# A two-layer decoder trunk on one core: the first hi row written by the modulating operation, and the rotary part of attention in fewer vector operations

## The chip, the cores and the metric

One core of a Trainium2 chip runs the whole program in one launch. The metric is device time in microseconds (us) of that core. TensorE (PE), VectorE (DVE), ScalarE (ACT) and GpSimd (POOL) each execute their own instruction list in order and wait for each other through semaphores; SyncE (SP) issues the DMA transfers.

## The reference, cut to what matters

256 tokens of width 1024 pass through two layers. Each layer is a SwiGLU FFN, a block of three attentions side by side (MLA with 6 heads, a sliding-window attention, a stick-breaking attention), and a second SwiGLU FFN. Ahead of each stands an RMS norm whose output is scaled and shifted by vectors that are computed from a conditioning vector. The part that the change touches is the MLA head preparation:

```python
h = modulate(x, norm_g[l, 0], sh1, sc1)              # rms_norm(x) * (1 + scale) + shift
...
qa = (rms_norm(c_q, q_a_norm[l]) @ w_uq[l]).reshape(B, S, MLA_HEADS, MLA_QK)   # 6 heads of 64 + 32
qa = rms_norm(qa, mla_q_norm[l])
qa = jnp.concatenate([qa[..., :MLA_NOPE], rope(qa[..., MLA_NOPE:], positions)], axis=-1)
kv = (rms_norm(c_kv, kv_a_norm[l]) @ w_ukv[l]).reshape(B, S, MLA_HEADS, MLA_NOPE + MLA_V)
k_pe_h = jnp.broadcast_to(k_pe[:, :, None, :], (B, S, MLA_HEADS, MLA_ROPE))
ka = rms_norm(jnp.concatenate([kv[..., :MLA_NOPE], k_pe_h], axis=-1), mla_k_norm[l])
ka = jnp.concatenate([ka[..., :MLA_NOPE], rope(ka[..., MLA_NOPE:], positions)], axis=-1)
```

`rope` turns the two halves (16 and 16) of the 32 rotary columns of a head by an angle: `[x1*cos - x2*sin, x2*cos + x1*sin]`.

## The kernel before, in words

The large matmuls run in three passes on pairs of tiles: an fp32 operand is split into a rounded "hi" part and the remainder "lo", and hi·hi, lo·hi and hi·lo are added up in PSUM (lines 243, 246 and 247, in `mm3`). The weights come in through SP as `raw`, ACT or DVE writes `hi` (line 230), DVE writes `lo` (line 234). The activations have their own pair: `hh` and `hl`, eight rows of 128 features by 256 tokens. Between its other work DVE forms the conditioning vectors, one 128x1024 product-and-sum after another (line 171).

A scheduler of the language decides the order of the instructions on each engine from the order in the program, the dependencies and its own estimate of durations; what is wrapped in `pin` keeps its place in program order. Two instructions of different engines that touch one PSUM tile are put one after the other, even where both only read.

**The opening** (lines 1205 to 1241) makes the first row of the first FFN's input: DVE multiplies row 0 of x by the norm factor (line 1236), applies scale and shift (1237), rounds the result to `hh[:, 0]` (1239), subtracts to get `hl[:, 0]` (1240), and copies the norm factor (1241). Then come the `lo` parts of the first weights (234) and the further rows, one by one, in `opening` (lines 451 to 462).

**Attention** first projects to the MLA latents. Line 797 multiplies to `kps`, the unscaled keys and values of all heads: four PSUM tiles, one for each block `b` of 128 tokens and each half `hf` of the heads. They take all four slots of the PSUM pool `mm`. ACT squares the key parts (844) and copies the value parts (855), DVE sums the squares (845), POOL takes the power -1/2 to get `rk` (848). DVE turns the shared rotary key `kpe` of each block by a call of `rope` (lines 832 to 838). Then, for each `b` and `hf`, PE makes three query heads of 96 columns in a PSUM tile (line 863), ACT copies the 64 plain columns to `qcat` (866), DVE turns the 32 rotary columns (four operations: 835 to 838), ACT squares all 96 columns (869) and DVE sums the squares (870). DVE then makes `rkn` (875), scales the plain keys into `kcat` (879; each of these four is the last reader of one tile of `kps`) and the rotary keys (880). DVE puts together the variance of the queries (884), POOL takes the power (886), DVE scales it (888). PE transposes `qcat` and `kcat` by heads (900) into tiles of the pool `mm`; ACT copies the queries out to `qT` (903), DVE the keys to `kT` (905). The scores of MLA (1058), and with them the rest of attention, follow. In both layers PE has one more projection (`stick_in(1, 4)`, 48 matmuls of lines 243 to 247) beside these steps.

Of the kernel before, what the change touches and what calls it, by code (L numbers as in the profile page):

```python
# [7 lines left out]
F32 = mybir.dt.float32  # L8
# [4 lines left out]
AF = mybir.ActivationFunctionType  # L13
ALU = mybir.AluOpType
AX = mybir.AxisListType

P = 128
# [36 lines left out]
def trunk_kernel(ctx: ExitStack, tc: tile.TileContext, x, c, posc, positions, cols_in, row, w_mod, w_gu1, w_down1, w_in,  # L54
                 w_small, w_out, w_gu2, w_down2, out):
    nc = tc.nc
    pin = tc.keep_in_program_order
    ACT, DVE, POOL, PE, SP = nc.scalar, nc.vector, nc.gpsimd, nc.tensor, nc.sync
# [19 lines left out]
    xa = res.tile([P, KD, T], F32, name="xa")  # L78
# [4 lines left out]
    hh, hl = (h[:, 0:KD * T].rearrange("p (k t) -> p k t", k=KD) for h in (h_hi, h_lo))  # L83
# [69 lines left out]
    modc = const.tile([P, 2, 9, 8], F32, name="modc")  # L153
# [491 lines left out]
    def attention(l, ap, aw, bg):  # L645
# [13 lines left out]
        def spread(a, n):  # L659
            return a.rearrange("p (h o) -> p h o", o=1).to_broadcast([P, a.shape[-1], n])  # L660

        def over_heads(a, n):
            return a.rearrange("p (o d) -> p o d", o=1).to_broadcast([P, n, a.shape[-1]])
# [83 lines left out]
        def stick_in(i, at):  # L747
            if C["L"][l]["U"][i] == at:
                banks[i] = [pacc(), pacc()]
                drain(unscaled(3328 + 2048 * i, (P, P), banks[i], 1))  # L750
                left = banks.copy()
                for j in left if len(left) == 2 else ():
                    stick_out(j)
                if len(outs) == 4:
                    norm(l, 1, rsb)
# [74 lines left out]
        ksq = ap.tile([P, 2, 6, 64], F32, tag="s5", name="ksq")  # L830

        def rope(dst, src, tb, n, nm):
            ta = aw.tile([P, n, 32], F32, tag="ropa" + nm, name="ropa")
            t2 = aw.tile([P, n, 32], F32, tag="ropb" + nm, name="ropb")
            DVE.tensor_tensor(ta, src, over_heads(tb[:, 0:32], n), op=ALU.mult)
            DVE.tensor_tensor(t2[:, :, 0:16], src[:, :, 16:32], over_heads(tb[:, 32:48], n), op=ALU.mult)
            DVE.tensor_tensor(t2[:, :, 16:32], src[:, :, 0:16], over_heads(tb[:, 48:64], n), op=ALU.mult)
            DVE.tensor_tensor(dst, ta, t2, op=ALU.add)

        kv = ap.tile([P, 2, 6], F32, name="kv")  # L840
        krs = []
        for b in range(2):
            for hf in range(2):
                ACT.activation(ksq[:, b, hf * 3:hf * 3 + 3], kps[2 * b + hf][:, :, 0:64], AF.Square)
# [1 line left out]
            DVE.tensor_scalar(kv[:, b], kss[:, b], lr2[:, 1, b:b + 1], kpss[:, b:b + 1], op0=ALU.mult, op1=ALU.add)  # L846
        rk = kv
        POOL.tensor_tensor(rk.rearrange("p b h -> p (b h)"), kv.rearrange("p b h -> p (b h)"), nhalf[:, 0:12], op=ALU.pow)
        for b in range(2):
            krs.append(aw.tile([P, 1, 32], F32, tag="kr", name="kr"))  # L850
            rope(krs[b], kpe[:, b:b + 1], ropet[:, l, 1, b], 1, "k")
        for b in range(2):
            for hf in range(2):
                hs = slice(hf * 3, hf * 3 + 3)
                ACT.activation(va[:, b, hs], kps[2 * b + hf][:, :, 64:128], AF.Copy, scale=lr[:, 1, b:b + 1])
        stick_in(0, 3)
        stick_in(1, 3)
        for b in range(2):
            for hf in range(2):
                hs = slice(hf * 3, hf * 3 + 3)  # L860
                qp = pacc()
                for k in range(2):
                    PE.matmul(qp[:, 0:288], cT[:, k, b * P:(b + 1) * P], wuq[:, k, hf * 288:(hf + 1) * 288],
                              start=k == 0, stop=k == 1)
                q3 = heads3(qp[:, 0:288])
                ACT.activation(qcat[:, b, hs, 0:64], q3[:, :, 0:64], AF.Copy)
                rope(qcat[:, b, hs, 64:96], q3[:, :, 64:96], ropet[:, l, 0, b], 3, "q")
                sq = aw.tile([P, 3, 96], F32, tag="pr", name="qsq")
                ACT.activation(sq, q3, AF.Square)
                DVE.tensor_reduce(qss[:, b, hs], sq, axis=AX.X, op=ALU.add)  # L870
                stick_in(0, 10 + 2 * b + hf)
                stick_in(1, 10 + 2 * b + hf)
        rkn = ap.tile([P, 2, 6], F32, name="rkn")
        for b in range(2):
            DVE.tensor_scalar(rkn[:, b], rk[:, b], lr[:, 1, b:b + 1], None, op0=ALU.mult)
        for b in range(2):
            for hf in range(2):
                hs = slice(hf * 3, hf * 3 + 3)
                DVE.tensor_tensor(kcat[:, b, hs, 0:64], kps[2 * b + hf][:, :, 0:64], spread(rkn[:, b, hs], 64), op=ALU.mult)
            DVE.tensor_tensor(kcat[:, b, :, 64:96], krs[b].to_broadcast([P, 6, 32]), spread(rk[:, b], 32), op=ALU.mult)  # L880

        qv = ap.tile([P, 2, 6], F32, name="qv")
        for b in range(2):
# [350 lines left out]
    pin(mod_tile(0, 0, 0, m0[:, 0]))  # L1234
    mod_finish(0, 0, 2, slice(0, 1))
    pin(DVE.tensor_tensor(xa[:, 0], xT[:, 0], rb, op=ALU.mult))
    pin(DVE.tensor_scalar(xa[:, 0], xa[:, 0], modc[:, 0, 1, 0:1], modc[:, 0, 0, 0:1], op0=ALU.mult, op1=ALU.add))
    rb0 = wk.tile([P, T], F32, tag="rsb", bufs=1, name="rsb")
    pin(DVE.tensor_copy(hh[:, 0], xa[:, 0]))
    pin(DVE.tensor_tensor(hl[:, 0], xa[:, 0], hh[:, 0].bitcast(F32), op=ALU.subtract))  # L1240
    pin(DVE.tensor_copy(rb0, rb))
    for l in range(DEPTH):
# [112 lines left out]
```

## Time and profile before

| | us |
|---|---|
| median of 3 runs | 1007.82 |
| lowest and highest of the 3 | 1006.34 and 1023.81 |
| the profiled execution, its own time | 1007.52 |
| span of the profiled execution | 1005.6 |

The rows further down come from the profiled execution: its span, 1005.6 us, runs from the first to the last instruction, and 1.9 us of its own time lie around it. Starts are counted from the start of the span. Where the text speaks of the spacing of two instructions it means start to start, since two neighbours on one engine can overlap a little.

### The profile page before, as it was taken

Reading aid. Unit: us, or ns where it says so; the run is one execution under the profiler, and the core shown is the slowest. Engines: PE = TensorE matmul, PEld = TensorE weight load, DVE = VectorE, ACT = ScalarE, POOL = GpSimd, SP = SyncE. Lnnn points to the kernel's source line nnn. Section 1 sums busy time; section 2 is a strip of 40 time slices with the busy share of each in tenths; the row PEclk is TensorE's granted clock in tenths of the full one; section 3 lists DMA queues with packets and bytes.
Section 4 is the critical chain, followed back from the end, with each engine's and each line's share of the span. In section 5 each row is a group of like instructions: output and inputs, shape, how many; then the busy total and the mean of one; then the engine's idle time right before and its main releaser. Section 6 shows DMA issues by size and latency. Waiting matters only on the chain.

```text
span 1005.6 us, 20450 instructions
## 1 busy us (share of the span) xinstructions
PE 983.7 (98%) x8396; PEld 957.1 (95%) x8396; DVE 792.2 (79%) x1422; ACT 533.3 (53%) x951; POOL 76.6 (8%) x123
## 2 busy tenths in 40 slices
PE   7999999998999999999999999999999999999998
PEld 6999999997888999999999999999988899999998
DVE  6999788898886898888789877777886678566663
ACT  4464345465755764444376444446575666444442
POOL 6001503002010000000000000000110000000000
PEclk9999999999999999999999999999999999999999
DMA  9988998654661679888866887772443146566631
GB/s 347 414 299 340 296 371 329 271 189 137 224 238 49 244 275 394 340 354 339 348 217 240 335 300 295 273 285 95 127 146 112 58 181 240 194 228 248 224 114 43
DMA packets 47936, 245.13 MB, mean 244 GB/s; under 512 B 4193, under 2 KB 4961, under 8 KB 29666
## 3 DMA queue, kind: packets, MB, share of 16 engines
q1 hardware_dynamic: 47840, 243.81, 64.9%
q8 instruction: 66, 1.08, 0.4%
q14 instruction: 28, 0.23, 0.1%
q10 hardware_dynamic: 2, 0.00, 0.0%
HBM read 242.69 MB, written 1.11 MB: 242 GB/s over the span
## 4 chain that ended last, share of the span: by engine, by line
PE 88%; DVE 7%; ACT 3%; POOL 1%; issue 1%; ACTq 0%; DVEq 0%; POOLq 0%
PE mm L243 16%; PE mm L246 16%; PE mm L247 16%; PE acc L246 11%; PE acc L243 11%; PE acc L247 11%; DVE lo L234 2%; DVE raw L171 1%; PE mm L1102 1%; PE mm L1082 1%; POOL qv L886 1%; PE mm L797 1%; PE mm L613 0%; PE mm L944 0%; PE mm L1143 0%
## 5 line engine op out<-in xcount | busy, mean ns | idle before, releaser
L234 DVE TENSOR_TENSOR lo<-raw,hi 128x1024 fp32r<-128x1024 f32 (+2 forms) x312 | 372.8, 1211 | 115.2 <-ACT hi L230 114.8
L230 ACT ACTIVATE hi<-raw 128x1024 fp32r<-128x1024 f32 (+1 forms) x296 | 306.5, 1048 | 201.9 <-PE mm L246 126.9
L246 PE MATMUL mm<-h_lo,hi 128*128 128x256 f32 (+1 forms) x1360 | 377.1, 278 | 0.0
L243 PE MATMUL mm<-h_hi,hi 128*128 128x256 f32 (+1 forms) x1360 | 376.8, 278 | 0.0
L247 PE MATMUL mm<-h_hi,lo 128*128 128x256 f32 (+1 forms) x1360 | 375.4, 277 | 0.0
L246 PEld LDWEIGHTS mm<-h_lo,hi 128*128 128x128 f32 x1360 | 254.8, 187 | 0.1
L243 PEld LDWEIGHTS mm<-h_hi,hi 128*128 128x128 f32 x1360 | 254.4, 188 | 0.3 <-ACT bias L620 0.2
L247 PEld LDWEIGHTS mm<-h_hi,lo 128*128 128x128 f32 x1360 | 254.0, 187 | 0.2
L243 PE MATMUL acc<-g,hi 128*128 128x256 f32 x682 | 188.9, 277 | 0.0
L247 PE MATMUL acc<-g,lo 128*128 128x256 f32 x682 | 188.9, 277 | 0.0
L246 PE MATMUL acc<-g,hi 128*128 128x256 f32 x682 | 188.7, 277 | 0.0
L171 DVE CUSTOM_DVE_ANT_0 raw<-raw,cond 128x1024 f32<-128x1024 f32 x144 | 172.2, 1220 | 0.0
L247 PEld LDWEIGHTS acc<-g,lo 128*128 128x128 f32 x682 | 128.2, 188 | 0.1
L243 PEld LDWEIGHTS acc<-g,hi 128*128 128x128 f32 x682 | 128.2, 188 | 0.0
L246 PEld LDWEIGHTS acc<-g,hi 128*128 128x128 f32 x682 | 128.0, 188 | 0.0
L243 PE MATMUL acc<-h_hi,hi 128*128 128x256 f32 (+1 forms) x288 | 79.8, 291 | 4.5 <-ACT h_hi L461 1.7
L246 PE MATMUL acc<-h_lo,hi 128*128 128x256 f32 (+1 forms) x288 | 80.5, 285 | 0.2
L247 PE MATMUL acc<-h_hi,lo 128*128 128x256 f32 (+1 forms) x288 | 79.3, 283 | 0.0
L448 ACT ACTIVATE g<-gg 128x256 fp32r<-128x256 f32 x82 | 34.0, 417 | 60.9 <-DVE gg L447 60.8
L445 ACT ACTIVATE sg<-mm 128x256 f32<-128x256 f32 x78 | 29.4, 377 | 59.5 <-PE mm L247 58.9
L243 PEld LDWEIGHTS acc<-h_hi,hi 128*128 128x128 f32 x288 | 53.2, 191 | 6.3 <-ACT h_hi L461 1.9
L246 PEld LDWEIGHTS acc<-h_lo,hi 128*128 128x128 f32 x288 | 54.9, 192 | 0.9 <-DVE h_lo L732 0.6
(307 smaller groups left out, 1122.8 us busy)
## 6 DMA issues: line engine op xcount, KB each, us to landing
raw<-in_dram SPq DMA_DIRECT2D x218, 1024.0 KB, 6.1
raw<-in_dram SPq DMA_DIRECT2D x4, 832.0 KB, 7.3
raw<-in_dram SPq DMA_DIRECT2D x4, 768.0 KB, 4.7
raw<-in_dram SPq DMA_DIRECT2D x4, 512.0 KB, 6.7
far<-relm SPq DMA_DIRECT2D x8, 256.0 KB, 11.4
small<-in_dram SPq DMA_DIRECT2D x2, 960.0 KB, 6.0
xT<-in_dram SPq DMA_DIRECT2D x4, 256.0 KB, 4.2
out_dram<-xT SPq DMA_DIRECT2D x3, 256.0 KB, 2.3
```

Source lines behind the costliest of these rows:

```text
L171: return DVE.tensor_tensor_reduce(w, w, cond, 1.0, 0.0, ALU.mult, ALU.add, modc[:, l, v, d:d + 1])
L230: t = DVE.tensor_copy(hi, r) if on[i:i + 1] == "d" else ACT.activation(hi, r, AF.Copy)
L234: t = DVE.tensor_tensor(lo, r, hi.bitcast(F32), op=ALU.subtract)
L243: t = PE.matmul(o, wh, ah, start=start, stop=False)
L246: PE.matmul(o, wh, al, start=False, stop=False)
L247: PE.matmul(o, wl, ah, start=False, stop=stop)
L445: ACT.activation(sg, banks[t][:, 0:T], AF.Silu)
L448: behind[0] = ACT.activation(g[:, 0], gg, AF.Copy).ins
L797: PE.matmul(kp[:, 0:384], cT[:, 2, b * P:(b + 1) * P], wukv[:, hf * 384:(hf + 1) * 384], start=True, stop=True)
L886: POOL.tensor_tensor(rq, qv, nhalf[:, 0:12].rearrange("p (a b) -> p a b", a=2), op=ALU.pow)
L1082: PE.matmul(opv[:, i * 64:(i + 1) * 64], pT[:, j * P:(j + 1) * P], va[:, kb, h0 + i], start=kb == 0, stop=kb == b)
L1102: PE.matmul(sp[:, i * P:(i + 1) * P], win["q"][rr, i, b * P:(b + 1) * P], ksT[rr, kb * P:(kb + 1) * P], start=True, stop=True)
```

## The change

In the opening a DVE operation with the same two factors now writes `hh[:, 0]` straight from the normalized row, and the second one writes `xa[:, 0]` as before; the copy that rounded `xa[:, 0]` to `hh[:, 0]` is gone. In attention the two calls of `rope` for the shared key become one call over both blocks; ACT copies all 96 columns of the three query heads to `qcat` and squares them into one tile per block; after the second half of a block, one call of `rope` turns the six heads in place in `qcat`, and one sum covers six heads. `rkn` is one operation instead of two.

```diff
         def rope(dst, src, tb, n, nm):
-            ta = aw.tile([P, n, 32], F32, tag="ropa" + nm, name="ropa")
-            t2 = aw.tile([P, n, 32], F32, tag="ropb" + nm, name="ropb")
-            DVE.tensor_tensor(ta, src, over_heads(tb[:, 0:32], n), op=ALU.mult)
-            DVE.tensor_tensor(t2[:, :, 0:16], src[:, :, 16:32], over_heads(tb[:, 32:48], n), op=ALU.mult)
-            DVE.tensor_tensor(t2[:, :, 16:32], src[:, :, 0:16], over_heads(tb[:, 48:64], n), op=ALU.mult)
+            ta = aw.tile([P, n, 32], F32, tag="ropa" + nm, bufs=1, name="ropa")
+            t2 = aw.tile([P, n, 32], F32, tag="ropb" + nm, bufs=1, name="ropb")
+            DVE.tensor_tensor(ta, src, tb[:, :, 0:32], op=ALU.mult)
+            DVE.tensor_tensor(t2[:, :, 0:16], src[:, :, 16:32], tb[:, :, 32:48], op=ALU.mult)
+            DVE.tensor_tensor(t2[:, :, 16:32], src[:, :, 0:16], tb[:, :, 48:64], op=ALU.mult)
             DVE.tensor_tensor(dst, ta, t2, op=ALU.add)
...
-        for b in range(2):
-            krs.append(aw.tile([P, 1, 32], F32, tag="kr", name="kr"))
-            rope(krs[b], kpe[:, b:b + 1], ropet[:, l, 1, b], 1, "k")
+        krs = aw.tile([P, 2, 32], F32, tag="kr", bufs=1, name="kr")
+        rope(krs, kpe, ropet[:, l, 1], 2, "k")
...
+        qsq = [ap.tile([P, 768], F32, tag=t, name="qsq")[:, 0:576].rearrange("p (h d) -> p h d", h=6) for t in ("s3", "s5")]
...
                 q3 = heads3(qp[:, 0:288])
-                ACT.activation(qcat[:, b, hs, 0:64], q3[:, :, 0:64], AF.Copy)
-                rope(qcat[:, b, hs, 64:96], q3[:, :, 64:96], ropet[:, l, 0, b], 3, "q")
-                sq = aw.tile([P, 3, 96], F32, tag="pr", name="qsq")
-                ACT.activation(sq, q3, AF.Square)
-                DVE.tensor_reduce(qss[:, b, hs], sq, axis=AX.X, op=ALU.add)
+                ACT.activation(qcat[:, b, hs], q3, AF.Copy)
+                ACT.activation(qsq[b][:, hs], q3, AF.Square)
+                if hf:
+                    rope(qcat[:, b, :, 64:96], qcat[:, b, :, 64:96], over_heads(ropet[:, l, 0, b], 6), 6, "q")
+                    DVE.tensor_reduce(qss[:, b], qsq[b], axis=AX.X, op=ALU.add)
...
-        for b in range(2):
-            DVE.tensor_scalar(rkn[:, b], rk[:, b], lr[:, 1, b:b + 1], None, op0=ALU.mult)
+        DVE.tensor_tensor(rkn, rk, spread(lr[:, 1], 6), op=ALU.mult)
...
-            DVE.tensor_tensor(kcat[:, b, :, 64:96], krs[b].to_broadcast([P, 6, 32]), spread(rk[:, b], 32), op=ALU.mult)
+            DVE.tensor_tensor(kcat[:, b, :, 64:96], over_heads(krs[:, b], 6), spread(rk[:, b], 32), op=ALU.mult)
...
     pin(DVE.tensor_tensor(xa[:, 0], xT[:, 0], rb, op=ALU.mult))
+    pin(DVE.tensor_scalar(hh[:, 0], xa[:, 0], modc[:, 0, 1, 0:1], modc[:, 0, 0, 0:1], op0=ALU.mult, op1=ALU.add))
     pin(DVE.tensor_scalar(xa[:, 0], xa[:, 0], modc[:, 0, 1, 0:1], modc[:, 0, 0, 0:1], op0=ALU.mult, op1=ALU.add))
     rb0 = wk.tile([P, T], F32, tag="rsb", bufs=1, name="rsb")
-    pin(DVE.tensor_copy(hh[:, 0], xa[:, 0]))
     pin(DVE.tensor_tensor(hl[:, 0], xa[:, 0], hh[:, 0].bitcast(F32), op=ALU.subtract))
     pin(DVE.tensor_copy(rb0, rb))
```

## Rows read from the trace of the kernel before

**Rows 1.** The page: the span, and the busy time of each engine over it with its share and its count of instructions.

```profile
span 1005.6 us, 20450 instructions
...
PE 983.7 (98%) x8396; PEld 957.1 (95%) x8396; DVE 792.2 (79%) x1422; ACT 533.3 (53%) x951; POOL 76.6 (8%) x123
```

**Rows 2.** Who PE waited for, over the whole span: the line that waited, the line it waited for, us in total, how often, the longest.

```profile
PE mm L900 <- DVE kcat L879: 3.6, 1, 3.6
...
PE mm L1058 <- DVE kT L905: 1.6, 1, 1.6
...
PE acc L1018 <- DVE kn L1013: 0.4, 1, 0.4
```

**Rows 3.** The timeline of DVE and of PE in layer 0's attention, where the heads are prepared: start, duration, line, operation, count; in brackets the idle time ahead and what ended it.

```profile
239.44 0.61 PE L900 MATMUL mm<-ident,qcat 128*96 128x128 f32 x4 [3.57 <-DVE kcat L879]
...
234.82 0.24 DVE L835 TENSOR_TENSOR ropa<-acc,ropet 128x96 f32<-128x96 f32 x1
...
235.88 0.45 DVE L870 TENSOR_REDUCE qss<-qsq 128x3 f32<-128x288 f32 x1
236.25 0.20 DVE L837 TENSOR_TENSOR ropb<-acc,ropet 128x48 f32<-128x48 f32 x1
236.36 0.25 DVE L835 TENSOR_TENSOR ropa<-acc,ropet 128x96 f32<-128x96 f32 x1
236.53 0.25 DVE L838 TENSOR_TENSOR qcat<-ropa,ropb 128x96 f32<-128x96 f32 x1
...
238.94 0.35 DVE L879 TENSOR_TENSOR kcat<-mm,rkn 128x192 f32<-128x192 f32 x1
239.21 0.44 DVE L870 TENSOR_REDUCE qss<-qsq 128x3 f32<-128x288 f32 x1
...
240.10 0.62 DVE L879 TENSOR_TENSOR kcat<-mm,rkn 128x192 f32<-128x192 f32 x2
240.63 0.35 DVE L880 TENSOR_TENSOR kcat<-kr,kv 128x192 f32<-128x192 f32 x1
240.89 0.36 DVE L884 TENSOR_SCALAR qv<-qss,lr 128x6 f32<-128x6 f32 x2
241.16 1.22 DVE L171 CUSTOM_DVE_ANT_0 raw<-raw,cond 128x1024 f32<-128x1024 f32 x1
...
244.54 0.36 DVE L888 TENSOR_SCALAR qv<-qv,lr 128x6 f32<-128x6 f32 x2 [2.15 <-POOL qv L886]
```

**Rows 4.** The timelines of ACT and of POOL in the same stretch.

```profile
233.67 1.36 ACT L855 ACTIVATE va<-mm,lr 128x192 f32<-128x192 f32 x4 [0.34 <-POOL lr L816]
...
236.48 0.41 ACT L869 ACTIVATE qsq<-acc 128x288 f32<-128x288 f32 x1 [0.24 <-DVE ropb L837]
237.59 0.41 ACT L869 ACTIVATE qsq<-acc 128x288 f32<-128x288 f32 x1 [0.69 <-DVE ropb L837]
...
234.50 2.43 POOL L848 TENSOR_TENSOR kv<-kv,nhalf 128x12 f32<-128x12 f32 x1 [0.86 <-DVE ropb L837]
241.33 3.17 POOL L886 TENSOR_TENSOR qv<-qv,nhalf 128x12 f32<-128x12 f32 x1 [4.40 <-DVE qv L884]
```

**Rows 5.** Busy time by stretch in layer 0's attention: the stretch, its length, then busy us (and instructions) of PE, PEld, DVE, ACT and POOL, the granted clock of PE as a share of full speed, the DMA share and GB/s.

```profile
239.50:244.30 4.80, 4.61 (x25) 3.81 (x25) 2.89 (x10) 1.80 (x3) 2.97 (x1) 0.64 0.02 7
...
241.00:241.50 0.50, 0.50 (x4) 0.45 (x4) 0.50 (x3) 0.00 (x0) 0.17 (x1) 0.50 0.00 0
...
244.30:262.00 17.70, 17.70 (x134) 15.74 (x132) 17.46 (x36) 11.95 (x34) 0.53 (x2) 1.00 0.51 168
```

**Rows 6.** The same transposes of line 900 in the timeline of PE, four in layer 0 and four in layer 1.

```profile
242.77 1.06 PE L900 MATMUL mm<-ident,qcat 128*96 128x128 f32 x4
...
732.04 0.60 PE L900 MATMUL mm<-ident,qcat 128*96 128x128 f32 x4
```

**Rows 7.** Layer 1, the same steps in the timelines of DVE, POOL and PE.

```profile
731.19 0.36 DVE L884 TENSOR_SCALAR qv<-qss,lr 128x6 f32<-128x6 f32 x2
...
731.63 2.44 POOL L886 TENSOR_TENSOR qv<-qv,nhalf 128x12 f32<-128x12 f32 x1 [4.80 <-DVE qv L884]
...
734.10 0.36 DVE L888 TENSOR_SCALAR qv<-qv,lr 128x6 f32<-128x6 f32 x2 [2.16 <-POOL qv L886]
734.37 1.88 DVE L905 COPY kT<-mm 96x512 f32<-96x512 f32 x3
...
736.39 1.10 PE L1058 MATMUL mm<-kT,qT 96*128 96x256 f32 x4 [1.64 <-DVE kT L905]
```

**Rows 8.** All instructions of a line over the span: count, then ns of the shortest, median and longest, first and last start in us.

```profile
L845 DVE TENSOR_REDUCE kss<-ksq x4: 532/542/547, 230.1 to 723.0; 128x6 f32<-128x384 f32 x4
```

**Rows 9.** The timeline of DVE in the opening, and under it two starts of PE's first three-pass matmuls.

```profile
13.72 0.41 DVE L1237 TENSOR_SCALAR xa<-xa,modc 128x256 f32<-128x256 f32 x1
14.17 0.29 DVE L1239 CAST h_hi<-xa 128x256 fp32r<-128x256 f32 x1
14.50 0.43 DVE L1240 TENSOR_TENSOR h_lo<-xa,h_hi 128x256 fp32r<-128x256 f32 x1
14.84 0.42 DVE L1241 COPY rsb<-acc 128x256 f32<-128x256 f32 x1
...
14.61 0.98 PE L243 MATMUL acc<-h_hi,hi 128*128 128x256 f32 x3 [1.38 <-DVE h_hi L1239]
...
30.76 0.74 PE L243 MATMUL acc<-h_hi,hi 128*128 128x256 f32 x4 [1.74 <-ACT h_hi L461]
```

More of the change, by code (lines that the diff above doesn't have):

```diff
@@ L832, in rope @@
         def rope(dst, src, tb, n, nm):
-            ta = aw.tile([P, n, 32], F32, tag="ropa" + nm, name="ropa")
-            t2 = aw.tile([P, n, 32], F32, tag="ropb" + nm, name="ropb")
-            DVE.tensor_tensor(ta, src, over_heads(tb[:, 0:32], n), op=ALU.mult)
-            DVE.tensor_tensor(t2[:, :, 0:16], src[:, :, 16:32], over_heads(tb[:, 32:48], n), op=ALU.mult)
-            DVE.tensor_tensor(t2[:, :, 16:32], src[:, :, 0:16], over_heads(tb[:, 48:64], n), op=ALU.mult)
+            ta = aw.tile([P, n, 32], F32, tag="ropa" + nm, bufs=1, name="ropa")
[3 more added lines that the diff above has]
+            DVE.tensor_tensor(t2[:, :, 16:32], src[:, :, 0:16], tb[:, :, 48:64], op=ALU.mult)
             DVE.tensor_tensor(dst, ta, t2, op=ALU.add)
         kv = ap.tile([P, 2, 6], F32, name="kv")
-        krs = []
         for b in range(2):
```

## The prediction

> **What bounds the kernel now.** I read the page first, then the list of PE's waits, then the timelines around the two longest waits in attention, and last the opening. The page shows a kernel bound by PE: it is busy 983.7 of 1005.6 us [rows 1]. So no more than 21.9 us can be won by anything that leaves PE's own work alone, and the change leaves it alone: the matmuls, their shapes and their number stay. The list of PE's waits tells which idle time the change can reach. In attention these are line 900, the first transposes of the heads, 3.6 us behind `kcat` on DVE (layer 0), and line 1058, the first MLA scores, 1.6 us behind `kT` on DVE (layer 1) [rows 2]. The edited lines stand right ahead of both on DVE.
>
> The timeline of layer 0 tells why. The first transposes write to a tile of the pool `mm`, whose four slots `kps` holds; the first slot comes free when line 879 has read it, at 238.94 + 0.35 = 239.29, and PE starts at 239.44 [rows 3]. Line 879 comes that late because DVE and ACT take turns on each query tile in PSUM: ACT's square (869) starts when DVE's line 837 has read the tile, DVE's sum (870) waits for the square, and the next tile's line 837 stands behind that sum. One such round lasts 1.1 us: the squares start at 236.48 and 237.59 [rows 4], each ended wait naming line 837.
>
> After the keys DVE runs line 884 at 240.89, POOL takes 3.17 us for the power [rows 4], and DVE stands still 2.15 us for it ahead of line 888 at 244.54 [rows 3]. From 244.3 to 262.0 DVE is busy 17.46 of 17.70 us [rows 5], and its backlog sets PE's next wait, line 1018 behind `kn` [rows 2]. So what counts in layer 0 is when line 884 runs. In layer 1 the same steps show it directly: 884 at 731.19, the power until 734.07, 888, the three copies to `kT` until 736.25, line 1058 at 736.39 after 1.64 us of idle PE [rows 7].
>
> **The change part by part: the opening.** One operation of 0.29 us (1239) goes, one like line 1237 (0.41 us) comes [rows 9]. `hh[:, 0]` starts at 13.72 instead of 14.17 and ends at 14.13 instead of 14.46, so PE's first matmul can start about 0.33 us earlier than 14.61. What follows on DVE gains nothing: line 1237 comes second and doesn't depend on the first write; two neighbours without a dependency are 0.34 apart (1240 to 1241), two with one 0.45 (1237 to 1239). That gives 14.06 for `xa` and 14.51 for `hl`, against 14.50 now [rows 9]. DVE runs the chain that follows, and PE waits for it again at 30.76 (1.74 us, line 461) [rows 9], so PE's 0.33 us become a longer wait there. Bounds: 0.33 us won, if PE's start did set the end; 0.12 lost, if the second operation starts at the full 0.45. I take 0, the row of DVE's chain being the nearest.
>
> **The rotary part, per layer.** DVE goes from 30 instructions (8 for the shared key, 16 for the queries, 4 sums, 2 for `rkn`) to 15 (4, 8, 2, 1). Nothing crosses SP's queue, and no DMA is issued earlier or later in program order. For their price I take spacings. A 128x96 product is 0.17 apart (line 835 at 236.36 to line 838 at 236.53), a 128x192 product 0.27 (line 879 twice from 240.10, next at 240.63) [rows 3]. A turn of six heads is two of 192 elements and two of 96: 2 x 0.27 + 2 x 0.17 = 0.88 us. The sum over 576 elements no row shows: the one over 288 takes 0.45 and is 0.37 apart from the next [rows 3], the one over 384 takes 0.54 [rows 8]. By that slope (0.09 for 96) 576 elements are 0.37 + 3 x 0.09 = 0.64; bounds 0.64 and, in proportion to the elements, 0.54 x 1.5 = 0.81. I take 0.65.
>
> ACT decides when DVE can begin. Its four copies to `va` run from 233.67 to 235.03, four in 1.36 us, or about 0.31 apart [rows 4]. The first half's copy and square fit ahead of them; behind come three copies and three squares of 288 elements, 0.41 long as the squares are now [rows 4] and also taken as 0.31 apart. The second half's copy of block 0 then ends at 235.03 + 0.41 = 235.44, the last copy of block 1 at 236.7, the last square at 237.0. ACT pays 0.07 us more per copy (0.41 against 0.34), hidden since DVE is behind it from here on.
>
> DVE: turn of block 0 from 235.5, its sum at 236.38, turn of block 1 at 237.03, its sum at 237.91, `rkn` at 238.56, line 879 at 238.7. Now it is 238.94, so PE's first transposes come only 0.25 us earlier: the rounds with ACT are gone, but the turn starts at 235.5 instead of 234.82 [rows 3], since it waits for both halves, and both sums stand ahead of line 879, while now the last one (0.37) comes after it. That last point returns at line 884: from the first line 879 to it are 1.95 us now, 1.58 without the sum, so 884 starts at 240.28 instead of 240.89: 0.6 us earlier. POOL's power and line 888 move with it, and DVE's backlog up to line 1018. Layer 1 has the same operations in the same order; I take 0.6 there too, off the 1.64 us ahead of line 1058.
>
> One rule is weighed here, as to the power on POOL that both layers wait for. The rows show 3.17 us for line 886 in layer 0, where line 171 runs beside it on DVE from 241.16, and 2.44 in layer 1 [rows 3, 4, 7]. The Trainium skill (GPSIMD Engine Reference, Key points) says that GpSimd shares its SBUF interfaces with VectorE and is disturbed by VectorE instructions with two SBUF inputs; line 171 is one, so the rows fit. By that rule the power for `rk` (2.43 us) now runs beside turns that read two SBUF tensors, where line 835 read PSUM. If it grows to the 3.17 us of the other row it ends at 237.67, still ahead of `rkn` at 238.56: no change. Whether line 171 keeps its place behind line 884 is open; without it 0.73 us more would be won in layer 0, which I keep for the lower end.
>
> **The sum.** The profiled execution took 1007.52 us, 0.3 under the median of the runs. 0 - 0.6 - 0.6 = -1.2 gives 1006.3 for it, and 1006.6 for the median. About 2% (20 us) is what a measurement of this kernel can tell from no change; the forecast lies far inside.
>
> **The rivals.**
>
> *PE keeps its clock.* After the idle 3.57 us the granted clock is 0.50 of full speed (1.2 of 2.4 GHz) at 241.0, and on average 0.64 over 239.5 to 244.3 [rows 5]; four transposes last 1.06 us there against 0.60 in layer 1 [rows 6], where PE had not idled. At full speed the 4.8 us would give (1 - 0.64) x 4.8 = 1.7 us back. The Trainium skill (TensorE: Matmul & The Clock Gate, Part 1) says that idling throttles the clock and that the moment depends on where the kernel falls in the monitor's own time; the trace agrees on the fall, and by that a wait that is only 0.25 us shorter may go either way. For it: a shorter wait. Against it: 17.46 us of DVE work in the next 17.70 [rows 5] make PE wait at line 1018 instead, so most of it would not reach the end. With all of it the median is 1004.9.
>
> *A new wait eats it.* DVE gains 0.6 us, but another partner ends the wait, and PE idles as long as before, in total: 1007.8. For it: 0.25 us only at line 900. Against it: line 888 does nothing for 2.15 us but wait for POOL, so an earlier 884 must show.
>
> *The change makes it slower.* The turn of a block needs both halves' copies, which stand behind `va` on ACT. If all of ACT's query work goes there and does not overlap, the second copy of block 0 ends at 235.03 + 3 x 0.41 = 236.26; turns at full durations (2 x 0.35 + 2 x 0.25 = 1.2) and sums of 0.81 put `rkn` at 236.3 + 4.0 = 240.3 and line 884 at about 242.0: 1.1 us later than now, and 1.1 in layer 1: 1010.0. It decides once the first line 879 of layer 0 starts after 240.89 - 1.58 = 239.3. For it: DVE has nothing of the queries to do from about 234.6 until the copies are there. Against it: the rows overlap everywhere.
>
> *The scheduler rearranges what follows.* Its estimates shift, so anything behind can change order. The largest single PE wait in attention, 3.6 us [rows 2], is what I give to one such new or vanished wait: 1004.2 or 1011.4.
>
> **How the numbers follow.** Forecast 0.42, clock kept 0.12, new wait 0.18, slower 0.18, rearranged 0.10. The range reaches down to 1003.5 (the forecast less the 1.7 of the clock, the 0.73 of the power and the 0.33 of the opening is 1003.8) and up to the slower rival's 1010.0; the forecast alone spans 1005.5 to 1007.5. Faster by over 2% would need nearly all idle time of PE: 0.01. Slower by over 2% needs a rearrangement of five times the size above: 0.01. Within 2%: 0.98.
>
> **What would show it.** Right: no ACT square waits for line 837's successor; line 884 at about 0.6 us earlier relative to the `va` copies in both layers; PE's wait for line 900 at 3.3 us, for 1058 at 1.0; in the opening PE's first hi matmul 0.3 us earlier and `hl` where it was. Wrong: line 879 starting later after `va` than now, line 884 unmoved, a granted clock of 1.00 right behind line 900, or PE waits of over 1 us at lines that have none now.

## The result, and the profile after

The changed kernel takes 1019.67 us (median of 4 runs, 1017.8 to 1027.12) where the kernel before takes 1014.9 beside it (4 runs, 1006.34 to 1023.81): ratio 1.0104, 95% interval 1.0056 to 1.0153. It is slower, by about 1%, and the forecast of 1006.6 with its range of 1003.5 to 1010.0 missed it. Runs of the kernel before spread from about 1005 to 1028 over all rounds below, those of the changed kernel from 1009 to 1027, and the time follows the mean granted clock of PE; the ratios leave out runs that lie over 1.5% above the fastest of their kernel, so the tables below also give means over all runs.

The profiled execution of the changed kernel took 1017.8 us. Its page, span and busy time (to [rows 1]):

```profile
span 1016.1 us, 20410 instructions
...
PE 990.9 (98%) x8396; PEld 963.9 (95%) x8396; DVE 791.3 (78%) x1392; ACT 532.2 (52%) x951; POOL 79.8 (8%) x123
```

DVE has its 30 instructions less, and PE is 7.2 us longer busy with the same 8396 matmuls: first sign that the matmuls themselves ran slower somewhere. PE's waits (to [rows 2]; line 898 is 900 of before, 1056 is 1058, 1016 is 1018):

```profile
PE mm L898 <- DVE kcat L877: 4.4, 2, 4.2
...
PE mm L898 <- DVE kT L903: 1.0, 1, 1.0
PE mm L1056 <- DVE kT L903: 0.9, 1, 0.9
...
PE acc L1016 <- DVE kn L1011: 0.7, 1, 0.7
```

The wait for the keys is longer, not shorter, a second one behind it is new, and the one in layer 1 is 0.7 shorter. The timelines of DVE, ACT, POOL and PE in layer 0 (to [rows 3, 4, 6]) show why:

```profile
231.74 0.16 DVE L818 SCALAR_TENSOR_TENSOR lr<-lr 128x4 f32<-128x4 f32 x1 [0.83 <-POOL lr L816]
...
232.55 1.22 DVE L171 CUSTOM_DVE_ANT_0 raw<-raw,cond 128x1024 f32<-128x1024 f32 x1
...
233.84 0.34 DVE L835 TENSOR_TENSOR ropa<-qcat,ropet 128x192 f32<-128x192 f32 x1
...
234.44 0.74 DVE L869 TENSOR_REDUCE qss<-qsq 128x6 f32<-128x576 f32 x1
235.11 0.34 DVE L838 TENSOR_TENSOR qcat<-ropa,ropb 128x192 f32<-128x192 f32 x1
235.37 0.74 DVE L869 TENSOR_REDUCE qss<-qsq 128x6 f32<-128x576 f32 x1
...
236.72 0.35 DVE L878 TENSOR_TENSOR kcat<-kr,kv 128x192 f32<-128x192 f32 x1
236.99 0.35 DVE L838 TENSOR_TENSOR qcat<-ropa,ropb 128x192 f32<-128x192 f32 x1
237.25 1.14 DVE L877 TENSOR_TENSOR kcat<-mm,rkn 128x192 f32<-128x192 f32 x4
...
238.58 0.36 DVE L882 TENSOR_SCALAR qv<-qss,lr 128x6 f32<-128x6 f32 x2
...
242.22 0.36 DVE L886 TENSOR_SCALAR qv<-qv,lr 128x6 f32<-128x6 f32 x2 [2.15 <-POOL qv L884]
242.49 0.68 DVE L903 COPY kT<-mm 96x512 f32<-96x512 f32 x1
243.09 1.21 DVE L171 CUSTOM_DVE_ANT_0 raw<-raw,cond 128x1024 f32<-128x1024 f32 x1
...
244.23 1.28 DVE L903 COPY kT<-mm 96x512 f32<-96x512 f32 x2
...
232.97 0.43 ACT L865 ACTIVATE qcat<-acc 128x288 f32<-128x288 f32 x1
...
232.51 3.38 POOL L847 TENSOR_TENSOR kv<-kv,nhalf 128x12 f32<-128x12 f32 x1 [0.81 <-DVE kv L845]
239.01 3.17 POOL L884 TENSOR_TENSOR qv<-qv,nhalf 128x12 f32<-128x12 f32 x1 [3.12 <-DVE qv L882]
...
237.75 1.06 PE L898 MATMUL mm<-ident,qcat 128*96 128x128 f32 x4 [4.24 <-DVE kcat L877]
...
243.23 1.09 PE L898 MATMUL mm<-ident,kcat 128*96 128x128 f32 x4 [1.01 <-DVE kT L903]
```

A product-and-sum for the conditioning vectors (line 171, 1.22 us) now stands ahead of the first query turn. Before, DVE turned the first half there. Another L171 stands between the first copy to `kT` and the other two, and PE waits 1.01 us for those. All transposes ran at 1.06 to 1.09 us for four, the slow value of [rows 6].

Stretches with the granted clock (columns as in [rows 5]), after first, then the kernel before on the same 100 matmuls as in the line 300 to 322:

```profile
236.00:247.00 11.00, 8.25 (x39) 7.53 (x40) 8.17 (x25) 2.63 (x5) 3.17 (x1) 0.53 0.31 112
300.00:322.00 22.00, 21.42 (x100) 19.68 (x100) 9.83 (x29) 6.43 (x21) 0.70 (x1) 0.53 0.12 45
...
302.00:304.00 2.00, 2.00 (x11) 2.00 (x11) 0.84 (x1) 0.48 (x1) 0.00 (x0) 0.50 0.34 143
```

```profile
298.38:311.30 12.92, 12.34 (x100) 11.38 (x100) 8.21 (x25) 6.67 (x22) 0.70 (x1) 1.00 0.18 74
```

This is the largest item. From about 301 to 322 us, a stretch that begins in the products of probabilities and values, PE is at 0.50 of full speed (1.2 of 2.4 GHz): 22.0 us for 100 matmuls that took the kernel before 12.9 us at 1.00. It is "busy" all along, so no list of waits shows it; only the clock column does. PE had waited 1.4 us for ACT (line 1072) just ahead of it, but the kernel before waits 1.3 us at that place too and keeps the clock.

Layer 1 (to [rows 7]) and the opening (to [rows 9]) of the changed kernel:

```profile
741.49 0.36 DVE L882 TENSOR_SCALAR qv<-qss,lr 128x6 f32<-128x6 f32 x2
...
744.40 0.36 DVE L886 TENSOR_SCALAR qv<-qv,lr 128x6 f32<-128x6 f32 x2 [2.16 <-POOL qv L884]
744.67 1.87 DVE L903 COPY kT<-mm 96x512 f32<-96x512 f32 x3
...
746.69 1.10 PE L1056 MATMUL mm<-kT,qT 96*128 96x256 f32 x4 [0.90 <-DVE kT L903]
...
13.48 0.42 DVE L1234 TENSOR_TENSOR xa<-xT,acc 128x256 f32<-128x256 f32 x1 [0.24 <-PE acc L275]
13.94 0.42 DVE L1235 TENSOR_SCALAR h_hi<-xa,modc 128x256 fp32r<-128x256 f32 x1
14.40 0.41 DVE L1236 TENSOR_SCALAR xa<-xa,modc 128x256 f32<-128x256 f32 x1
14.85 0.43 DVE L1238 TENSOR_TENSOR h_lo<-xa,h_hi 128x256 fp32r<-128x256 f32 x1
...
31.11 0.72 PE L243 MATMUL acc<-h_hi,hi 128*128 128x256 f32 x4 [1.74 <-ACT h_hi L461]
```

PE's starts at fixed points of the program split the span into stages. The table gives each stage's length minus that of the kernel before, in us, for the profiled executions of the changed kernel (`after`, and `after2` and `after3`, the same code again) and of the two halves of its attention edit (`a_l0`, `a_l1`, below).

| stage | after | after2 | after3 | a_l0 | a_l1 |
|---|---|---|---|---|---|
| opening, from the first product of row 0 to the start that was 30.76 | +0.14 | +0.12 | +0.12 | +0.01 | 0 |
| first FFN of layer 0 | -2.69 | -2.70 | +0.41 | -1.13 | -2.70 |
| query products to first transposes | +0.67 | +1.82 | +1.78 | +1.44 | +0.47 |
| to the projection behind them | +1.37 | +1.03 | +1.03 | +1.03 | -0.47 |
| to the first scores | +1.22 | -0.01 | 0 | 0 | -0.01 |
| line 1018 to the second FFN | +9.92 | +10.75 | +1.43 | +10.59 | +1.07 |
| layer 1: query products to first scores | -0.58 | -0.57 | -0.56 | 0 | -0.57 |

The row of the first FFN differs even between executions of the same code (`after2`, `after3`) and says nothing of the change (last section). Behind the first scores of layer 1 these profiles are 0.1 (`after`) to 2.7 us longer than the kernel before; all but `after` have one more stretch at half clock there.

### The profile page after: what moved, and what is told of

Read it like the earlier page. It is cut to its first block, busy times and chain, and to the rows that moved or that the text cites. A ratio compares the mean times of both kernels' runs of the same rounds, so it can differ in the third digit from the quotient of the medians.

```text
span 1016.1 us, 20410 instructions
## 1 busy us (share of the span) xinstructions
PE 990.9 (98%) x8396; PEld 963.9 (95%) x8396; DVE 791.3 (78%) x1392; ACT 532.2 (52%) x951; POOL 79.8 (8%) x123
## 4 chain that ended last, share of the span: by engine, by line
PE 87%; DVE 8%; ACT 3%; POOL 1%; issue 1%; DMA 0%; ACTq 0%; POOLq 0%; DVEq 0%
PE mm L243 15%; PE mm L247 15%; PE mm L246 15%; PE acc L246 11%; PE acc L247 11%; PE acc L243 11%; DVE raw L171 2%; DVE lo L234 1%; PE mm L942 1%; PE mm L1100 1%; PE mm L1080 1%; ACT hi L230 1%; POOL qv L884 1%; PE mm L1141 1%; PE mm L797 1%
## 5 line engine op out<-in xcount | busy, mean ns | idle before, releaser
L171 DVE CUSTOM_DVE_ANT_0 raw<-raw,cond 128x1024 f32<-128x1024 f32 x144 | 172.2, 1221 | 0.0
```

Source lines behind the costliest of these rows:

```text
L171: return DVE.tensor_tensor_reduce(w, w, cond, 1.0, 0.0, ALU.mult, ALU.add, modc[:, l, v, d:d + 1])
```

## Experiments

The experiments were timed in five rounds (12 runs each, `e_rope` 6). "Mean" is the mean over all runs minus that of the kernel before in the same round; "clock" is the part of it that the mean granted clock makes, with each run's loss taken as (1 - clock) times its time; the last column counts runs with a mean clock of 0.985 or less. All five profiled executions with such a clock have one half-clock stretch of 20.5 us near 301 us; of the others, all at 0.990 or more, none has it. In runs without a profile the low clock stands for that stretch; no profile covers 0.986 to 0.989.

| kernel | median | ratio, 95% interval | mean | clock | low runs |
|---|---|---|---|---|---|
| before (all rounds) | 1012.9 | | | | 46 of 151 |
| after (first result) | 1019.7 | 1.0104, 1.0056 to 1.0153 | +6.1 | | 3 of 4 |
| after2 | 1017.8 | 1.0076, 1.0039 to 1.0113 | +3.8 | +3.0 | 4 of 12 |
| after3 | 1018.0 | 1.0037, 0.9996 to 1.0077 | +3.2 | +3.4 | 5 of 12 |
| e_open | 1011.2 | 1.0008, 0.9959 to 1.0057 | -1.0 | -1.5 | 2 of 12 |
| e_rope | 1019.6 | 1.0113, 1.0048 to 1.0177 | +6.3 | +2.5 | 3 of 6 |
| e_k | 1011.9 | 0.9978, 0.9935 to 1.0020 | -1.2 | -0.5 | 3 of 12 |
| e_q | 1017.3 | 1.0009, 0.9957 to 1.0061 | +6.9 | +5.2 | 6 of 12 |
| a_l0 | 1021.4 | 1.0077, 1.0036 to 1.0117 | +5.4 | +4.9 | 7 of 12 |
| a_l1 | 1009.5 | 0.9975, 0.9936 to 1.0014 | -3.8 | -3.3 | 1 of 12 |
| a_fix | 1012.4 | 1.0007, 0.9960 to 1.0054 | 0.0 | +0.8 | 3 of 12 |
| a_sum | 1012.7 | 1.0005, 0.9964 to 1.0046 | +1.2 | -1.0 | 0 of 12 |
| a_rq | 1013.4 | 1.0003, 0.9957 to 1.0049 | +2.9 | +1.4 | 3 of 12 |
| w_before | 1013.3 | 0.9997, 0.9963 to 1.0030 | -0.3 | -2.1 | 0 of 12 |
| w_after | 1016.9 | 1.0044, 1.0009 to 1.0079 | +2.3 | -1.2 | 0 of 12 |
| w_fix | 1012.8 | 0.9990, 0.9956 to 1.0024 | -1.3 | -3.7 | 0 of 12 |
| b_rq | 1007.9 | 0.9961, 0.9915 to 1.0006 | -1.1 | 0.0 | 2 of 12 |
| b_l1 | 1008.7 | 0.9964, 0.9921 to 1.0006 | -3.5 | -1.7 | 1 of 12 |
| b_l1b | 1012.7 | 1.0008, 0.9965 to 1.0050 | -2.8 | -2.1 | 2 of 12 |

The means carry about ±2.5 to ±5 us (twice their standard error; the four runs of the first result ±10), so single rows decide little; groups of them do.

**Which part of the change?** `after2` is the changed kernel again. `e_open` is the kernel before with the opening's edit alone, `e_rope` the changed kernel with the opening of before:

```diff
+    pin(DVE.tensor_scalar(hh[:, 0], xa[:, 0], modc[:, 0, 1, 0:1], modc[:, 0, 0, 0:1], op0=ALU.mult, op1=ALU.add))
...
-    pin(DVE.tensor_copy(hh[:, 0], xa[:, 0]))
```

> The changed kernel itself once more, beside the kernel before. Theory A (the clock): its trace shows PE at half clock from 301 to 322 us, in layer 0's attention, and for 10 us behind the first transposes of the heads; whether the clock falls differs from run to run in both kernels, so single runs of this kernel should come at about 1006 with a mean clock near 0.998 as well as at 1017 to 1022 with 0.98, and the kernel before should show both values too. Theory B (the order of instructions): the rearranged order itself costs the 10 us, so every run is at 1017 or above, whatever its clock, and the kernel before stays near 1007.

> The kernel before with the edit of the opening alone. By the traces the second operation in the opening starts 0.46 us after the first and not 0.34, so the cost is 0.1 to 0.4 us: theories A and B both expect the times of the kernel before, 1006.5 to 1008 where the clock holds. Only a theory that puts the loss into the opening (another start of PE that shifts the clock for all that follows) expects 1017 or more here in every run.

> The changed kernel with the opening of the kernel before: the attention part alone. Theory B expects what the changed kernel shows, 1017 to 1022, in every run. Theory A expects a mixture as in the changed kernel: 1005 to 1008 where the mean clock is near 0.998, 1017 to 1022 where it is 0.98. In the trace both expect PE's wait at the first transposes of layer 0 at 4.2 us, as in the changed kernel and not 3.6.

`after2` fits neither theory whole: not every run is at 1017 or above, and none comes near 1006. The highest mean clock in 28 runs of the changed kernel is 0.995; 47 of 151 runs of the kernel before have 0.996 or more. The opening alone changes nothing in the times that can be measured; the attention edit alone is as slow as the whole, though `e_rope`'s profile is 6.15 us longer in an FFN outside the change (last section). `e_k` keeps of it the merged turn of the shared key only, `e_q` is the changed kernel without that merge and with two operations for `rkn`:

```diff
-        rope(krs, kpe, ropet[:, l, 1], 2, "k")
+        for b in range(2):
+            rope(krs[:, b:b + 1], kpe[:, b:b + 1], over_heads(ropet[:, l, 1, b], 1), 1, "k")
```

> The kernel before with one part of the change alone: the shared key of both blocks turned by one call. It leaves the turns of the queries as they were. If the queries' turns by block bring the loss (theory A2), this runs as the kernel before: median 1011 to 1014, single runs down to 1006, wait at the first transposes 3.4 to 3.6 us. If any shift of the order on DVE costs 5 us (theory B), the median is 1016 or more.

> The changed kernel with the shared key's turn made per block and the two operations for the scaling of the keys back as in the kernel before: the opening edit and the merged query turns stay. Theory (the merged query turns alone shift the work ahead of the first transposes of layer 0, so that the clock falls more often): as slow as the changed kernel, 1016 to 1020 against about 1014 of the kernel before, lost clock time (share of missing clock times the time) 11 to 16 us on the mean against 9. Rival (the slowdown needs all parts of the attention edit, since it is a matter of the scheduler's order): within 2 us of the kernel before. Rival (chance of the clock in the earlier runs of the changed kernel): 1013 to 1015.

The key's merge alone is neutral. `e_q` has a median 8 us above the kernel before beside it and low runs in 6 of 12, but its interval holds 1, so it isn't shown to be slower. With `a_l0` below, that leaves the merged query turns as the likeliest part to carry the loss; no run shows it of them alone.

**Which layer?** `a_l0` and `a_l1` are the kernel before with the whole attention edit in one layer only; `after3`, the changed kernel, ran on the same chip:

```diff
+        new = l == 0
...
+                if new:
+                    ACT.activation(qcat[:, b, hs], q3, AF.Copy)
+                    ACT.activation(qsq[b][:, hs], q3, AF.Square)
```

> The kernel before with the attention edit in layer 0 alone (opening and layer 1 as before). Theory (the loss is made in layer 0: the gap on VectorE is filled with a product-and-sum of 1.2 us, both sums stand ahead of the keys, and the low-load stretch near 301 us follows in the same layer): 0.5 to 1.5 us more from the query projection to the first MLA scores, layer 1 as before, mean 2 to 6 us over the kernel before, the long half-clock stretch in 4 to 7 of 12 runs against about 3 of 12 of the kernel before. Rival (the loss is spread, or comes from the opening's 0.44 us and layer 1): mean within 2 us of the kernel before.

> The kernel before with the attention edit in layer 1 alone. Theory: layer 1 gains 0.55 to 0.6 us between the query projection and the first MLA scores (0.33 and 0.25 in the changed kernel), layer 0 as before, long half-clock stretch as often as in the kernel before (about 3 of 12), mean within 2 us of the kernel before. Rival (the edit costs in either layer): mean 2 to 6 us over the kernel before.

> The changed kernel once more, on the chip of its two halves. Theory (the clock's stretch falls more often): mean 3 to 5 us over the kernel before, the long half-clock stretch in 4 to 7 of 12 runs. Rival (the direct cost alone: 0.44 us of the opening, some 1 to 2 in layer 0, 0.6 back in layer 1): mean 1 to 2 us over the kernel before, the stretch in about 3 of 12.

Layer 0 alone is slower (interval above 1), layer 1 alone is not, and by the stage table gains the same 0.57 us as in the changed kernel. Its mean of -3.8 lies outside the 2 us that were expected either way; the clock makes 3.3 of it. PE's waits and the stretch of the values' products in `a_l0` repeat those of the changed kernel:

```profile
PE mm L925 <- DVE kcat L904: 5.0, 1, 5.0
...
PE mm L925 <- DVE kT L930: 1.0, 1, 1.0
```

```profile
301.00:323.00 22.00, 21.42 (x101) 19.67 (x100) 9.81 (x29) 6.89 (x23) 0.70 (x1) 0.53 0.12 47
```

**Which wait in layer 0?** `a_sum` puts the two sums behind the keys, `a_rq` scales the queries' factors behind the copies to `kT`, `a_fix` does both:

```diff
-                    DVE.tensor_reduce(qss[:, b], qsq[b], axis=AX.X, op=ALU.add)
...
+        for b in range(2):
+            DVE.tensor_reduce(qss[:, b], qsq[b], axis=AX.X, op=ALU.add)
```

```diff
-        for b in range(2):
-            DVE.tensor_scalar(rq[:, b], rq[:, b], lr[:, 0, b:b + 1], 96.0 ** -0.5, op0=ALU.mult, op1=ALU.mult)
...
+        for b in range(2):
+            DVE.tensor_scalar(rq[:, b], rq[:, b], lr[:, 0, b:b + 1], 96.0 ** -0.5, op0=ALU.mult, op1=ALU.mult)
```

> The changed kernel with two moves in the program: the two sums of squares of the queries after the keys are scaled, and the last scaling of the query factor (which waits for the power on POOL) after the copies of the transposed heads. Theory A2 (the change lengthens PE's idle time in layer 0, two waits of 4.2 and 1.0 us in place of one of 3.6, and PE's clock falls for more of the run because of it): PE waits under 3 us at the first transposes and not for the copies to kT, half clock near 240 us for 3.4 us or not at all, and the median comes to 1012 or less (changed kernel 1018, before 1013). Theory B (it is the rearranged order in the later part of attention that costs): the time stays at 1017 to 1020, since that part is as in the changed kernel.

> The changed kernel with its two sums of the query squares (576 elements each) put behind the keys; the scaling of the queries' factors stays ahead of the transposes. Theory (the sums stand ahead of the keys, 1.4 us, and the first transposes of layer 0 wait for it): the wait at the first transposes falls from 4.2 to about 3 us, and the median by 3 to 5 us to that of the kernel before. Rival (the wait for the power on GpSimd, with the copies to kT behind it, is what counts): the longer wait stays, the power starts 1.4 us later and the median stays at 1016 to 1020.

> The changed kernel with only the scaling of the queries' factors put behind the copies to kT; the sums stay where they are, ahead of the keys. Theory of the sums: no change in the first wait, 4.2 us; the second wait, 1.0 us for kT, goes; the median falls by 1 us or less, to 1016 to 1019. Rival (the wait for kT behind GpSimd's power breaks PE's run of work a second time and so holds the clock low): the stretch at half clock around the transposes of layer 0 ends by 244 instead of 246.7, and the median falls by 3 to 5 us. In layer 1 the wait ahead of the first MLA scores, 1.1 us, goes under both.

The start of `a_sum`'s first transposes, with its first wait, and DVE's own wait ahead of its keys, then in `a_rq` the last transposes and the projection behind them, with no second wait:

```profile
237.72 0.42 PE L899 MATMUL mm<-ident,qcat 128*96 128x128 f32 x1 [3.19 <-DVE kcat L876]
...
236.60 0.17 DVE L872 TENSOR_TENSOR rkn<-kv,lr 128x12 f32<-128x12 f32 x1 [1.41 <-POOL kv L847]
```

```profile
244.50 1.06 PE L895 MATMUL mm<-ident,kcat 128*96 128x128 f32 x4
245.22 0.50 PE L243 MATMUL acc<-h_hi,hi 128*128 128x258 f32 x1
```

A weight transfer ahead of this stage lands at different times in different profiles; in the changed kernel ACT waits for it and passes the delay on through lines 786 and 818:

```profile
221.45 1.06 ACT L230 ACTIVATE hi<-raw 128x1024 fp32r<-128x1024 f32 x1 [1.17 <-DMA raw<-in_dram]
```

Line 818 runs 1.95 us behind the first query product in the kernel before, 2.38 in the changed one, and 3.71 in `b_rq`, whose code is that of before up to there; so the delay is not the change's. With it taken out, the first transposes come 0.24 us later than before in `after`, `after2`, `e_rope`, `a_l0` and `a_rq` (0.23 in `after3`), 0.43 later in `e_q`, 0.46 earlier in `a_sum` and `a_fix`, and within 0.03 of before in `e_open`, `a_l1`, `b_l1` and `b_rq`. The sums ahead of the keys thus cost 0.70 us, and moving line 886 takes the second wait away. With the sums gone DVE stands still 1.41 us for POOL's power for `rk` (line 847), so that is the next limit. But `a_fix`, expected to shorten the wait in its profile, shows 4.2 us at the first transposes, since its transfer came 1.04 us late. The three are low in 6 of 36 runs, as rarely as kernels without the edit, and `a_sum` bears out its theory (first wait 3.2 us, median 1012.7); the median of `a_rq`, 1013.4, lies under the 1016 to 1019 that the theory of the sums gave it. Whether either move alone wins back the whole loss isn't settled: their means of +1.2 and +2.9 carry errors of 2.4 and 4.2.

**The clock in the values' products.** `w_before`, `w_after` and `w_fix` are the kernel before, the changed one and `a_fix` with products of 128 instead of 64 columns in MLA and the sliding-window attention; the other 64 columns go unused:

```diff
-                o = opv[:, i * 64:(i + 1) * 64]
-                PE.matmul(o, pT3[:, i], vs[:, b, rr], start=True, stop=b == 0)
+                o = opv[:, i * P:(i + 1) * P]
+                PE.matmul(o, pT3[:, i], vs[:, b], start=True, stop=b == 0)
```

> The changed kernel with wider products of probabilities and values in MLA and the window attention: 128 columns move instead of 64 (the upper 64 are not used), which leaves the count of matmuls the same and takes no longer where the weight load of 0.11 us is what counts. If the clock falls at 301 us because PE does little per us there (theory A with that reason), PE does more here and the half-clock stretch of 20 us is shorter or gone: 1005 to 1010. If PE's load in this stretch has nothing to do with it, the stretch stays and the time too: 1017 to 1022.

> The kernel before with the wider products alone. The kernel before had 7 of 29 runs with a mean clock of 0.985 or lower. Theory A with its reason: none here, median 1009 to 1012, and the best runs at 1005 to 1006 as before. Otherwise: some runs at 0.985 and below, median 1013.

> The kernel of a_fix with the wider products of probabilities and values (128 columns move, the upper 64 unused). Theory A with its reason (PE does too little per us from 296 us on, and the clock falls for 20 us in some runs): no run with a mean clock of 0.985 or lower, the highest time under 1018, median 1008 to 1011. If the clock there does not hang on PE's load: as many runs at 0.985 as in a_fix.

None of 36 runs is low, so the long stretch hangs on these products; which property of them counts isn't shown, since the edit changes the order of the work behind them too. It brings no time, and no median comes down to what was expected: the profile of `w_before` shows a wait that the kernel before does not have, and with the clock's part taken out the three are 1.8 to 3.5 us over the kernel before.

```profile
PE mm L728 <- DVE xa L723: 3.4, 2, 2.6
```

**A version that the rows point to.** `b_rq` is the kernel before with line 888 behind the copies to `kT`; `b_l1` does it in layer 1 alone, and `b_l1b` repeats that.

```diff
+        if l == 1:
+            for b in range(2):
+                DVE.tensor_scalar(rq[:, b], rq[:, b], lr[:, 0, b:b + 1], 96.0 ** -0.5, op0=ALU.mult, op1=ALU.mult)
```

> The kernel before with only the scaling of the queries' factors put behind the copies to kT, so that DVE doesn't stand still for GpSimd ahead of them. Theory (these waits cost what the rows say): in layer 1 the wait of 1.64 us ahead of the first MLA scores goes, layer 0 gains nothing, 1 to 1.6 us faster than the kernel before. Rival (the scaling lands behind other work of DVE and the values wait for it): 0 to 2 us slower.

> The kernel before with the scaling of the queries' factors behind the copies to kT in layer 1 alone. Theory: the wait of 1.6 us ahead of the first MLA scores of layer 1 goes, nothing else changes, 1.6 to 1.8 us faster than the kernel before on the mean of the runs at like clock. Rival (a shift of order in layer 0 takes it back): within 0.5 us.

> b_l1 once more, to tell 1.7 us (what its layer 1 shows) from nothing. Theory: mean and median 1 to 4 us below the kernel before. Rival (its first runs were lucky with the clock): within 1 us.

The wait of 1.64 us ahead of layer 1's first scores [rows 7] is gone in `b_l1`, and the stage is 1.79 us shorter:

```profile
734.71 1.03 PE L1062 MATMUL mm<-kT,qT 96*128 96x256 f32 x4
```

The medians of all three lie below the changed kernel's. That either beats the kernel before is not shown: every interval holds 1.

## Why the prediction was wrong

**The starting point.** The forecast was counted from 1007.82, the median of three runs. Over 151 more runs the kernel before has a median of 1012.9, outside the range too. So about 5 of the 13 us between forecast and result are the spread of the kernel before and not the change.

**The opening: 0 taken, +0.12 measured.** The sum failed at the spacing of the two operations that read `xa`: I took 0.34, and it is 0.46 (13.94 to 14.40). PE's first matmul comes 0.31 us sooner after the row's first product (1.03 against 1.34) and, as forecast, that is lost by the wait at line 461; the end pays the 0.12 that stood there as the upper bound.

**Layer 0: -0.6 taken, +1.27 measured at the transposes.** This is the step that failed. ACT did what was forecast: the second half's copy of block 0 ends at 233.40, 3.6 us behind the first query product without the transfer's delay, against 3.7. But the wait for both halves, which I had priced only as a later start of the turn, is a gap in DVE's list when the order is made, and line 171 was put into it; the turn starts at 233.84 instead of 233.40. The sums' spacing is 0.67, near the 0.65 taken, but line 878 and the last turn's end stand ahead of the first line 877. Hence +0.24 instead of -0.25 at the transposes. No run takes that line 171 away, so its share is read from the timeline and not tested. It also runs beside POOL's power for `rk`: 3.38 us, ending at 235.89, still ahead of `rkn`, so that growth had no effect here, as forecast. Line 882 did come 0.38 us earlier (9.22 less the delay of 0.43, against 9.17 behind the first query product), where 0.6 was forecast. That gain met the second thing I had left open only for line 171 behind line 884: another one now splits the copies to `kT`, and PE waits 1.01 us for it. The stage is 1.03 us longer; in `a_rq`, where that wait is gone, it is 0.13 longer. Two of the prediction's signs of being wrong are there: the first key operation starts 5.51 us after the `va` copies began, against 5.27, and PE waits over 1 us where it had not waited.

**Layer 1: -0.6 taken, -0.57 measured.** Here no line 171 stands on DVE in this stretch, in either kernel, the order is the one I assumed, and the wait ahead of the first scores falls from 1.64 to 0.90.

Together the rows give +0.12 + 1.27 - 0.57 = +0.8 us where I had -1.2. The means over all runs, 1018.4 for the changed kernel (28 runs) and 1013.8 for the kernel before (151), differ by 4.6; the clock's part is 4.0 (13.3 against 9.3 us lost), what is left is 0.6, near the rows' 0.8 but with an error of 1.2 (twice its standard error).

**The clock** is 4.0 of the 4.6 us between the kernels. It was a rival that I priced only as a gain of 1.7 us near the transposes, with 0.12. It went the other way: a long stretch at half clock 60 us later, which costs 9.1 us where it occurs (22.0 against 12.9) and which no row of before could show, since its one profile is of an execution without it. Near the transposes the first profile of the changed kernel has 10.2 us at half clock against 3.4, but that isn't the change's: `after2`, `after3` and `a_l0` have 6.8, `e_rope` has 3.4, and `e_open`, with attention as before, has 6.8. Kernels with the merged query turns in layer 0 and nothing moved (`after`, `after2`, `after3`, `e_rope`, `e_q`, `a_l0`) are low in 28 of 58 runs; those with layer 0's attention as before (`before`, `e_open`, `a_l1`, `b_l1`, `b_l1b`) in 52 of 199. That is 48% against 26%, a difference of 22 points with a standard error of 7. By the runs that enter the ratios alone it is 22 of 52 against 30 of 174; with the runs at 0.986 to 0.989 counted as well, 38 of 58 against 62 of 199. The groups were formed after the results, but each count says the same: the change makes the long stretch more frequent; it does not make it appear.

The Trainium skill (TensorE: Matmul & The Clock Gate, Part 1) says that where a kernel falls in the monitor's own time changes from run to run. The trace agrees that it is not the code alone: `after2` has the stretch, `after3`, the same code, hasn't.

**The rival that the scheduler rearranges** is the mechanism that came true; I gave it 0.10 and the price of one wait, 3.6 us. The slower rival's point, a first key operation after 239.3, or 7.58 us behind the first query product, was not reached (7.46 without the delay), so its price didn't come into it. What stays open: whether and how the lost 1.3 us in layer 0 lead to a slower clock 60 us later, and so why moving the sums or the scaling brings the runs back.

## What to carry to other kernels

Fewer operations with a later start leave a hole in an engine's list, and a scheduler fills it with whatever is ready; so before pricing a merge, ask what long operation stands ready at that moment, and look whether the same merge meets such filler in the other layer. In a kernel bound by PE, read the granted clock by stretch in several executions before pricing anything: a stretch at half clock counts as busy and hides from every list of waits. Count a forecast from many runs of the kernel before, not from three. Time the halves of a change layer by layer when the first profile mixes a gain and a loss.

## What was not expected of the hardware

The same 101 matmuls, PE over 95% busy in both, took 12.9 us at 1.00 of the clock in one execution and 22.0 us at 0.53 in another of the same code. First `after3`, then `after2`:

```profile
303.30:316.20 12.90, 12.32 (x101) 11.36 (x101) 8.04 (x24) 6.71 (x23) 0.70 (x1) 1.00 0.20 77
```

```profile
301.00:323.00 22.00, 21.42 (x101) 19.67 (x100) 9.83 (x29) 6.88 (x23) 0.70 (x1) 0.53 0.12 46
```

And at a granted clock of 1.00 throughout, the second layer's first FFN runs at two speeds: 1405 matmuls in 165 us in `e_rope` and `e_k`, 1452 in the kernel before, 6.15 us over the stage, with nothing of the change in it; all other profiles run there as the kernel before does. First `e_rope`, then the kernel before:

```profile
530.00:695.00 165.00, 165.00 (x1405) 164.87 (x1405) 122.74 (x185) 78.97 (x116) 0.00 (x0) 1.00 0.71 265
```

```profile
525.00:690.00 165.00, 165.00 (x1452) 164.86 (x1452) 127.71 (x191) 82.23 (x120) 1.54 (x1) 1.00 0.72 270
```

The first FFN of layer 0 moves by up to 3.1 us from execution to execution (-2.70 to +0.41 in the stage table); in the execution with +0.41 part of it ran at half clock, in the kernel before and `after2` none. No run here tells why.
